# Eight modulation chunks of the second layer move into its mixing, and the dots between the gathers' begin and the gates get a larger share of each tile

## The chip, the cores and the metric

The kernel runs on one core of one Trainium2 chip. The metric is the device time of one execution in microseconds. The kernel before takes 1582.73 us, the median of three runs (1582.06 to 1584.29).

Five engines work side by side, each on a list of its own in a fixed order: PE (matrix products), DVE (vectors), ACT (functions of one argument, copies), POOL and SP (here both mostly send transfers). An instruction that waits holds everything behind it on its engine. Transfers sent by SP, ACT and POOL run in three queues, which the profile calls q1, q10 and q0.

## The reference, cut to what matters

Two layers work on 256 tokens of 1024 numbers. A layer mixes tokens, then sends each token to a few single-neuron experts:

```python
c_act = jax.nn.silu(c)
for l in range(DEPTH):                      # 2 layers
    mod = c_act @ w_ada[l] + b_ada[l]       # w_ada[l]: 1024 x 6144
    sh1, sc1, g1, sh2, sc2, g2 = split(mod, 6)
    h  = rms_norm(x, norm1_g) * (1 + sc1) + sh1
    x  = x + g1 * (mixers(h @ w_in) @ w_out)
    h2 = rms_norm(x, norm2_g) * (1 + sc2) + sh2
    # 8 heads choose 16 of 16384 experts for every token
    u   = expert_down[experts];  act = gelu(einsum('td,thkd->thk', h2, u))
    x   = x + g2 * einsum('thk,thkd->td', gate * act, expert_up[experts])
```

The modulation vector `mod` depends on `c` alone. In the kernel, `w_ada[l]` is 48 chunks ("columns") of 128x1024 numbers, 512 KB each; a chunk is multiplied by `c_act` and summed along its rows, which gives 128 entries of `mod`. Columns 24 to 31 are `sh2`.

## The kernel before, in words

A layer goes through four stages. **Mixing**: 16 chunks of `w_in` and 8 of `w_out` run through PE in split precision (a chunk becomes a high part on ACT and a low part on DVE, L270), and the small work of the mixers is placed between the chunks by a table. **Retrieval**: 16 chunks of `w_pq` give the scores, and DVE picks the best experts in many small steps, which reach into the next stage. **Down**: for the dense tokens (the first 168 in layer 0, the first 160 in layer 1) the kernel goes through all 128 tiles of `expert_down`, 8 matmuls a tile (L357). **Up**: 128 tiles of `expert_up` in the same way (L1173). Each tile is 512 KB.

The other 88 (layer 0) or 96 tokens (layer 1) don't take part in that. For them POOL gathers rows: one indirect transfer (`fetch`, L1074) brings 128 rows of `expert_down`, 512 KB, into a free place; DVE multiplies it with the tokens and sums ("dot", `dot`, L1084), which frees the place for the next gather. There is one dot for each of the 88 or 96. In the up stage the same happens with rows of `expert_up`, which DVE adds to sums ("add", `add_row`, L1097 and L1099). At the end of the up stage PE folds these sums into the result (`folds`, L1179), and DVE writes the new x (L392).

**The gates.** The dense tokens need a gate for each expert. Once the picks of a layer are known and normalised (DVE, L922 to L924), PE transposes them (L934), ACT and DVE turn them into `parts` and `picks` (L939 to L943), and then 42 groups in layer 0, 40 in layer 1, each of 4 tokens, follow: DVE compares (`compare`, L1107), ACT scales (`factors`, L1117 to L1123), PE multiplies (`gate_mm`, L1133), and DVE and ACT use the result (`gate_use`, L1143 and L1141). Two groups can be in work at a time: the compare of group g+2 stands on DVE behind the `gate_use` of group g. A group is started every second tile.

**The order of the work** in the down stage is written out by the loop over its 128 tiles, in the second half of `experts`. Before the picks are known, each tile gets a budget of small steps ("fills", `run_fill`). "Begin" is the tile at which the first picks are known and the gathers begin; "start" is the tile at which the first compares are issued (the gates follow FLUSH tiles later). From D_FIRST tiles behind begin each tile gets a share of dots, `due`: DOT_SLOW between begin and the end of the fills, DOT_FAST from there to start, DOT_RATE behind it. While the gathers run, the budget of fills is cut by 1.2 * DOT_SLOW. DVE's list is thus a mix of fills, dots and gate steps in the order in which this loop issues them, and it doesn't depend on when a gather lands.

**Transfers.** `Src.seq` lists all streamed chunks. SP sends half the tiles of the down and up stages and ACT the other half (kind "second"), into a ring of seven places (`RAW`, tile "raw"). Some tiles of the down stage are loaded early into places of their own (kind "early", `AHEAD_AT`). All 48 modulation chunks of layer 1 are "asides": SP loads them into six other buffers, and DVE dots them (`ada_chunk`, L227) when it comes to them. 40 of these, columns 0 to 39, come in the down and up stages of layer 0: six at tile 20 of the down stage, then one every five tiles of it (`ASIDES_AT`), and the last 18 spread over the up stage. The other eight come in the down stage of layer 1. SP also sends some tables for the mixing of layer 1 and reads x back (`x_dram`), both in the up stage of layer 0. POOL's queue holds the gathers.

**Places.** The dots and gathers use places of the arena that are free then. Places of "early" tiles join them when the tile is used (from `AHEAD_AT` 28 on); some of them must be given back when few fills are left (RETIRE).

Of the kernel before, what the change touches and what calls it, by code (L numbers as in the profile page):

```python
# [14 lines left out]
OP = mybir.AluOpType  # L15
# [4 lines left out]
S = 256  # L20
DC = 8
D = 1024
# [26 lines left out]
SETS_KNOWN = 22  # L49
D_FIRST = 8  # L50
DOT_SLOW = 0.3
DOT_RATE = (0.85, 0.92)
DOT_FAST = 1.6
RETIRE = 9
AHEAD_AT = (8, 12, 16, 36, 40, 44, 48, 52, 56, 60, 64, 68, 100, 28, 32)
# [3 lines left out]
AHEAD_FIRST = 4  # L59
ASIDES_AT = ((20,) * 6 + tuple(range(46, 125, 5)), (20,) * 6 + (60, 72))  # L60
ASIDES_UP = (4, 100)
F_FIRST = 4
F_LAST = 124
# [19 lines left out]
def hybrid_trunk(ctx: ExitStack, tc: tile.TileContext, x_in, c_in, vec_in, w_ada, w_in, w_out, w_pq,  # L83
# [118 lines left out]
    def dma_ahead(upto):  # L202
        while Src.loaded < min(upto, len(Src.seq)):
            kind, src, raw = Src.seq[Src.loaded]
            if kind == "aside":
                raw = stream.tile([P, D], F32, name="aside", tag=("hi", "lo")[Src.aside % 2], bufs=3)
                Src.aside += 1
            elif kind != "early":
                raw = stream.tile([P, D], F32, name="raw", tag="raw", bufs=RAW)
            if kind == "second":  # L210
                Src.later.append((Src.loaded, raw, src))
            else:
                nc.sync.dma_start(raw, src)
            raws[Src.loaded] = raw
            Src.loaded += 1
# [32 lines left out]
    def cast_step(late=None):  # L248
# [8 lines left out]
        Src.cast += 1  # L257
        if kind == "aside":
            Src.asides.append((k, lambda: ada_chunk(arg[0], arg[1], raw)))
# [46 lines left out]
    def mix(a, b, first=0, last=None):  # L306
        last = len(a) if last is None else last
        o, used = list(a[:first]), 0
        for n, t in enumerate(a[first:]):
            o.append(t)  # L310
            want = min(len(b), len(b) * (n + 1) // max(1, last - first))
            o += b[used:want]
            used = want
        return o + b[used:]

    def mats(src, layer, n, kind="mat"):
        return [(kind, src[layer, p], None) for p in range(n)]

    seq = []
    for layer in range(DEPTH):  # L320
# [3 lines left out]
        if layer == 0:  # L324
# [7 lines left out]
            body = first[:2] + body[:n] + first[2:] + mix(body[n:], ada(0, [2, 3, 4]))  # L332
        body += mix(tail[:6], ada(0, [5])) + tail[6:] if layer == 0 else tail
        seq += body + [("whole" if n in WHOLE_PQ else "mat", w_pq[layer, n], None) for n in range(16)]
        dn, un = ([t if n % 2 else ("second", *t[1:]) for n, t in enumerate(mats(w, layer, 128, "whole"))]
                  for w in (down, up))
        for n, at in enumerate(AHEAD_AT):
            dn[AHEAD_FIRST + n] = ("early", dn[AHEAD_FIRST + n][1], region(at * S, D))
        aside = ada(1, [0, 1, 2, 3, 4] if layer + 1 < DEPTH else [5], "aside")
        for n, at in reversed(tuple(enumerate(ASIDES_AT[layer]))):  # L340
            dn.insert(at, aside[n])
# [5 lines left out]
    for t in seq:  # L347
        Src.ring.append(Src.ring[-1] + was if Src.ring else 0)
        was = t[0] not in ("early", "aside")
    Src.ring.append(Src.ring[-1] + was)  # L350
# [657 lines left out]
    def experts(layer, rest):  # L1008
# [225 lines left out]
        for i in range(128):  # L1234
# [34 lines left out]
            if start is None:  # L1269
                run_fill(FILL_DOWN[layer] if begin is None else FILL_DOWN[layer] - 1.2 * DOT_SLOW)  # L1270
            if known:
# [29 lines left out]
            n = i - AHEAD_FIRST  # L1301
            if 0 <= n < len(AHEAD_AT) and AHEAD_AT[n] >= 28:
                assert not retired
                free.append(region(AHEAD_AT[n] * S, D))
                if AHEAD_AT[n] != KEPT:
                    passing.append(free[-1])
                fetch()
# [130 lines left out]
```

## Time and profile before

| what | value |
|---|---|
| median of three runs | 1582.73 us |
| the profiled execution's own time | 1584.51 us |
| its span in the trace | 1582.6 us |
| mean granted PE clock | 0.991 |
| busy share of PE, DVE, ACT, POOL | 97%, 63%, 30%, 31% |
| mean transfer rate over the span | 361 GB/s |

The stages of the profiled execution: the tiles of layer 0's down stage begin near 195 us, while DVE is still picking, and end at 509 us; its up stage runs to 824 us; in layer 1 the down stage begins near 985 us, and the up stage runs from 1286 to 1578 us.

In the profile's rows, times are in us from the span's start. A group of instructions is shown by line, engine, operation and tiles (out<-in), then busy time and mean ns of one, then the idle time of its engine just ahead of it and what ended that. A row of a timeline has start, duration, engine, line and operation, the number of instructions that it joins, and in brackets the idle time ahead of it with its releaser. In a table of windows the number in brackets behind a busy time is a count of instructions, PEclk is the granted clock of PE (1.00 is full speed), and the last two columns are the busy share of the transfer engines and the rate.

### The profile page before, as it was taken

To read this page: it belongs to the slowest core of one execution; us is meant where nothing else is said; L and a number is where in the kernel's file an instruction comes from. 1 tells how busy PE (TensorE), PEld (TensorE's weight loads), DVE (VectorE), ACT (ScalarE), POOL (GpSimd) and SP (SyncE) were. 2 spreads that over 40 slices of the span, in tenths; PEclk is the share of its full clock that TensorE was granted. 3 is DMA by queue.
4 is the path that set the end of the run, shared out by engine and by line. 5 is a ranking of instruction groups with operands and counts; after the bars stand their busy time and mean duration, and the time that the engine had idled before them with its cause. 6 is when DMAs were issued, how large, how long until landed. Compare 5 with 4: busy or idle time off the path is not lost.

```text
span 1582.6 us, 28957 instructions
## 1 busy us (share of the span) xinstructions
PE 1542.3 (97%) x11240; PEld 1505.1 (95%) x11240; DVE 1000.0 (63%) x2255; ACT 472.5 (30%) x1356; POOL 496.8 (31%) x424
## 2 busy tenths in 40 slices
PE   6999999999999999998999999999999999999997
PEld 5879999999999999998999899999999999999997
DVE  6778898677787444444337578877667754444434
ACT  2346313465553000000026663134656610000000
POOL 1000124334344434444200001245443334444441
PEclk9999999999999999999999999999999999999998
DMA  9998489999999999999955574899999999999995
GB/s 385 339 375 319 138 289 348 418 418 419 417 418 416 415 419 419 418 419 419 412 189 171 186 258 139 292 351 419 417 418 419 418 419 419 418 419 419 419 418 211
DMA packets 156681, 571.21 MB, mean 361 GB/s; under 512 B 18131, under 2 KB 18659, under 8 KB 155392
## 3 DMA queue, kind: packets, MB, share of 16 engines
q1 hardware_dynamic: 66096, 241.07, 39.7%
q0 software_dynamic: 55744, 202.36, 32.0%
q10 hardware_dynamic: 34704, 125.93, 19.9%
q8 instruction: 88, 1.44, 0.3%
q14 instruction: 49, 0.40, 0.1%
HBM read 564.02 MB, written 4.09 MB: 359 GB/s over the span
## 4 chain that ended last, share of the span: by engine, by line
PE 40%; DMA 38%; issue 8%; DVE 7%; POOL 4%; ACT 2%; ACTq 0%; POOLq 0%; SPq 0%; DVEq 0%
DMA arena<-in_up,arena 17%; PE acc L1173 17%; DMA arena<-in_down_rows,arena 12%; PE ch L357 9%; DMA spots<-in_down_rows,arena 3%; DMA raw<-in_up 3%; POOL arena L1074 3%; PE ch L359 2%; PE ch L360 2%; PE ch L361 2%; DVE raw L227 1%; DMA raw<-in_w_ada 1%; PE ch L446 1%; DVE arena L1084 1%; PE g L952 1%
## 5 line engine op out<-in xcount | busy, mean ns | idle before, releaser
L1173 PE MATMUL acc<-arena,raw 128*128 128x168 f32 (+1 forms) x4096 | 580.5, 305 | 9.0 <-DMA raw<-in_up 9.0
L1173 PEld LDWEIGHTS acc<-arena,raw 128*128 128x128 f32 x4096 | 577.6, 192 | 11.3 <-DMA raw<-in_up 11.2
L357 PE MATMUL ch<-arena,raw 128*128 128x168 f32 (+2 forms) x3776 | 560.7, 307 | 0.1
L357 PEld LDWEIGHTS ch<-arena,raw 128*128 128x128 f32 x3776 | 536.2, 190 | 5.6 <-issue 1.8
L1099 DVE SCALAR_TENSOR_TENSOR spots<-arena,spots 128x1024 f32<-128x1024 f32 x156 | 200.4, 1284 | 222.1 <-DMA arena<-in_up,arena 220.8
L1074 POOL DMA_INDIRECT arena<-in_up,arena x159 | 215.1, 1353 | 280.5 <-DMA arena<-in_up,arena 203.9
L1074 POOL DMA_INDIRECT arena<-in_down_rows,arena x151 | 178.3, 1181 | 242.9 <-DVE arena L1084 180.7
L1084 DVE SCALAR_TENSOR_TENSOR arena<-arena,spots 128x1024 f32<-128x1024 f32 x151 | 183.1, 1222 | 86.1 <-DMA arena<-in_down_rows,arena 79.6
L1117 ACT ACTIVATE arena<-arena,parts 128x128 f16<-128x128 f16 x164 | 64.6, 394 | 142.1 <-DVE arena L1107 102.5
L388 ACT ACT_TABLE_LOAD x6 | 7.7, 1283 | 284.9 <-PE acc L1173 284.8
L357 PE MATMUL ch<-arena 128*128 128x160 f32 (+2 forms) x544 | 86.0, 317 | 6.1 <-issue 3.6
L357 PEld LDWEIGHTS ch<-arena 128*128 128x128 f32 x544 | 79.8, 192 | 11.2 <-ACT arena L410 5.2
L1150 ACT ACTIVATE arena<-ch 128x336 f32<-128x336 f32 (+32 forms) x122 | 41.9, 343 | 149.4 <-PE ch L357 128.9
L227 DVE SCALAR_TENSOR_TENSOR aside<-aside,arena 128x1024 f32<-128x1024 f32 x48 | 58.6, 1220 | 43.9 <-DMA aside<-in_w_ada 43.8
L359 PE MATMUL ch<-hh,hi 128*128 128x256 f32 x288 | 82.6, 289 | 2.0 <-DVE arena L477 1.9
L360 PE MATMUL ch<-hh,lo 128*128 128x256 f32 x288 | 81.8, 284 | 0.0
L361 PE MATMUL ch<-hh,hi 128*128 128x256 f32 x288 | 81.7, 284 | 0.0
L270 DVE TENSOR_TENSOR lo<-raw,hi 128x1024 fp32r<-128x1024 f32 x42 | 51.2, 1225 | 37.3 <-ACT hi L277 36.3
L227 DVE SCALAR_TENSOR_TENSOR raw<-raw,arena 128x1024 f32<-128x1024 f32 x48 | 57.9, 1217 | 8.9 <-DMA raw<-in_w_ada 5.4
L1119 ACT ACTIVATE arena<-arena,parts 128x128 f16<-128x128 f16 x164 | 63.4, 387 | 0.0
L1123 ACT ACTIVATE arena<-arena,parts 128x128 f16<-128x128 f16 x164 | 63.4, 386 | 0.0
L1121 ACT ACTIVATE arena<-arena,parts 128x128 f16<-128x128 f16 x164 | 63.4, 386 | 0.0
(231 smaller groups left out, 1661.9 us busy)
## 6 DMA issues: line engine op xcount, KB each, us to landing
raw<-in_up SPq DMA_DIRECT2D x128, 512.0 KB
raw<-in_up ACTq DMA_DIRECT2D x128, 512.0 KB
raw<-in_down SPq DMA_DIRECT2D x114, 512.0 KB
raw<-in_down ACTq DMA_DIRECT2D x112, 512.0 KB
raw<-in_w_ada SPq DMA_DIRECT2D x48, 512.0 KB
aside<-in_w_ada SPq DMA_DIRECT2D x48, 512.0 KB
raw<-in_w_pq SPq DMA_DIRECT2D x32, 512.0 KB
arena<-in_down SPq DMA_DIRECT2D x30, 512.0 KB
```

The source lines that it names most:

```text
L227: nc.vector.scalar_tensor_tensor(raw, raw, 1.0, cact, op0=OP.mult, op1=OP.mult, accum_out=mods[layer][:, col:col + 1])
L357: nc.tensor.matmul(dst, hi[:, cols], k[0], start=start, stop=stop, **kw)
L359: nc.tensor.matmul(dst, hi[:, cols], k[0], start=start, stop=False, **kw)
L360: nc.tensor.matmul(dst, lo[:, cols], k[0], start=False, stop=False, **kw)
L361: nc.tensor.matmul(dst, hi[:, cols], k[1], start=False, stop=stop, **kw)
L1074: nc.gpsimd.indirect_dma_start(out=held[n], out_offset=None, in_=rows if n >= TS else down_rows[:, :], in_offset=bass.IndirectOffsetOnAxis ...
L1084: nc.vector.scalar_tensor_tensor(row, row, 1.0, R_DX[which(k)[0]], op0=OP.mult, op1=OP.mult, accum_out=R_DOTS[:, k:k + 1])
L1099: nc.vector.scalar_tensor_tensor(R_SUM[s], row, w, R_SUM[s], op0=OP.mult, op1=OP.add)
L1117: nc.scalar.activation(og[0][:, 0, i, :], oh[:, 0, i, :], AF.Copy, scale=parts[:, 0, t + i:t + i + 1])
L1119: nc.scalar.activation(og[1][:, 0, i, :], oh[:, 0, i, :], AF.Copy, scale=parts[:, 1, t + i:t + i + 1])
L1121: nc.scalar.activation(og[0][:, 1, i, :], oh[:, 1, i, :], AF.Copy, scale=parts[:, 0, t + 2 + i:t + 3 + i])
L1173: nc.tensor.matmul(acc[d // 2][:, (d % 2) * S:(d % 2) * S + T], u[:, d * P:(d + 1) * P], acts[:, i, :], start=i == 0 and d % 2 == 0, stop= ...
```

## The change: what it does

Columns 24 to 31 of layer 1 are no asides any more. They get the kind "inline" and stand in the list of layer 1's mixing, behind its chunks 10, 11 and 14. POOL sends them (L208 in the numbering of the change) into places of the arena, and DVE dots them there (L264) when the mixing comes to them. Two of them, columns 27 and 28, land in places that are free early, and their transfers come into POOL's list in the up stage of layer 0, behind 50 and 56 of its gathers; their dots stand on DVE among the adds, behind 46 and 47 of them. The other six come on POOL behind the last gather. On DVE column 24's dot stands ahead of the updates of x, 25's ahead of the reciprocal of the following norm and 26's behind it, and 29, 30 and 31 in the mixing.

The asides of layer 0 fall from 40 to 32: one every seven tiles of the down stage (18 there instead of 22) and 14 instead of 18 in the up stage.

The other numbers change the loop of the down stage, in both layers: DOT_SLOW from 0.3 to 0.9 dots a tile, D_FIRST from 8 to 7, RETIRE from 9 to 4, and two places fewer join the gathers (threshold 36 instead of 28). The fills keep their full budget until the first dots, and then it is 2.2 - 1.2 * 0.9 = 1.12 a tile in layer 0 instead of 2.2 - 0.36 = 1.84.

```diff
-D_FIRST = 8
-DOT_SLOW = 0.3
+D_FIRST = 7
+DOT_SLOW = 0.9
...
-RETIRE = 9
+RETIRE = 4
...
-ASIDES_AT = ((20,) * 6 + tuple(range(46, 125, 5)), (20,) * 6 + (60, 72))
+ASIDES_AT = ((20,) * 6 + tuple(range(46, 125, 7)), (20,) * 6 + (60, 72))
...
+MIXED = ((24, 10, 76), (25, 10, 80), (26, 10, 84), (27, 11, 29), (28, 11, 33), (29, 11, 37), (30, 11, 41), (31, 14, 17))
...
-            if kind == "aside":
+            if kind == "inline":
+                raw = raw[0]
+                nc.gpsimd.dma_start(raw, src)
+            elif kind == "aside":
...
-            else:
+            elif kind != "inline":
                 nc.sync.dma_start(raw, src)
...
-        if kind == "aside":
+        if kind == "inline":
+            view = (lambda v: v.rearrange("p (a b) -> p a b", a=2)) if len(raw.shape) == 3 else (lambda v: v)
+            nc.vector.scalar_tensor_tensor(raw, raw, 1.0, view(cact), op0=OP.mult, op1=OP.mult,
+                                           accum_out=mods[arg[1]][:, arg[2]:arg[2] + 1])
+            ada_end(arg[1], arg[2], 8)
+        elif kind == "aside":
...
+        body = [t for n, b in enumerate(body) for t in [b] + beside(layer, n)]
...
+        aside = [t for t in aside if t[2][1] not in apart]
...
-                run_fill(FILL_DOWN[layer] if begin is None else FILL_DOWN[layer] - 1.2 * DOT_SLOW)
+                if begin is None or i < begin + D_FIRST:
+                    run_fill(FILL_DOWN[layer])
+                elif fills[0]:
+                    run_fill(FILL_DOWN[layer] - 1.2 * DOT_SLOW)
+                else:
+                    run_aside()
...
-            if 0 <= n < len(AHEAD_AT) and AHEAD_AT[n] >= 28:
+            if 0 <= n < len(AHEAD_AT) and AHEAD_AT[n] >= 36:
```

What this does to the engines' lists is seen best in layer 1. Here is DVE's list of the kernel before around the normalisation of the picks (L922 to L924); L1084 is a dot, L902 to L912 are the last steps of the picking:

```order
L912 TENSOR_TENSOR arena<-arena 128x128
L902 TENSOR_TENSOR arena<-arena,iota_87 128x2048
L907 TENSOR_TENSOR arena<-arena 128x2048
L911 TENSOR_TENSOR arena<-arena 128x8x128
L911 TENSOR_TENSOR arena<-arena 128x8x64
L911 TENSOR_TENSOR arena<-arena 128x8x32
L912 TENSOR_TENSOR arena<-arena 128x128
L1084 SCALAR_TENSOR_TENSOR arena<-arena,spots 128x1024
L922 TENSOR_REDUCE arena<-arena 128x8
L923 RECIPROCAL arena<-arena 128x8
L924 TENSOR_TENSOR arena<-arena 128x128
```

And here is the same place after the change, where these lines have numbers higher by 22 (a dot is L1106):

```order
L924 TENSOR_TENSOR arena<-arena,iota_87 128x2048
L1085 TENSOR_SCALAR arena<-pairs 128x32
L1106 SCALAR_TENSOR_TENSOR arena<-arena,spots 128x1024
L929 TENSOR_TENSOR arena<-arena 128x2048
L1106 SCALAR_TENSOR_TENSOR spots,arena<-spots 128x1024
L1106 SCALAR_TENSOR_TENSOR arena<-arena,spots 128x1024
L933 TENSOR_TENSOR arena<-arena 128x8x128
L933 TENSOR_TENSOR arena<-arena 128x8x64
L933 TENSOR_TENSOR arena<-arena 128x8x32
L934 TENSOR_TENSOR arena<-arena 128x128
L1106 SCALAR_TENSOR_TENSOR arena<-arena,spots 128x1024 x2
L944 TENSOR_REDUCE arena<-arena 128x8
```

Dots now stand between the steps: in the whole list 18 dots come ahead of the normalisation of layer 1 instead of 3, and 16 instead of 3 in layer 0.

The second place is DVE's list up to the first `gate_use` (L1143) of layer 1, first before, from the compares (L1107) of the first two groups on:

```order
L1107 TENSOR_TENSOR arena<-iota_85,picks 128x1024 x2
L1084 SCALAR_TENSOR_TENSOR arena<-arena,spots 128x1024 x2
L227 SCALAR_TENSOR_TENSOR aside,mod_112<-aside,arena 128x1024
L1084 SCALAR_TENSOR_TENSOR arena<-arena,spots 128x1024 x6
L227 SCALAR_TENSOR_TENSOR aside,mod_112<-aside,arena 128x1024
L1084 SCALAR_TENSOR_TENSOR spots,arena<-spots 128x1024
L1084 SCALAR_TENSOR_TENSOR arena<-arena,spots 128x1024 x2
L1143 SCALAR_TENSOR_TENSOR arena<-arena,g 128x42x4
L1107 TENSOR_TENSOR arena<-iota_85,picks 128x1024
```

and after the change, where L1129 is a compare, L231 an aside's dot and L1165 a `gate_use`:

```order
L1129 TENSOR_TENSOR arena<-iota_85,picks 128x1024 x2
L1106 SCALAR_TENSOR_TENSOR arena<-arena,spots 128x1024 x4
L231 SCALAR_TENSOR_TENSOR aside,mod_112<-aside,arena 128x1024
L1106 SCALAR_TENSOR_TENSOR arena<-arena,spots 128x1024
L1106 SCALAR_TENSOR_TENSOR spots,arena<-spots 128x1024
L1106 SCALAR_TENSOR_TENSOR arena<-arena,spots 128x1024
L231 SCALAR_TENSOR_TENSOR aside,mod_112<-aside,arena 128x1024
L1106 SCALAR_TENSOR_TENSOR spots,arena<-spots 128x1024
L1106 SCALAR_TENSOR_TENSOR arena<-arena,spots 128x1024 x2
L1165 SCALAR_TENSOR_TENSOR arena<-arena,g 128x50x4
L1129 TENSOR_TENSOR arena<-iota_85,picks 128x1024
```

Counted from the layer's first dot, 32 dots stand ahead of the first `gate_use` of layer 1 instead of 19, and 28 instead of 18 in layer 0; the compare of the third group comes right behind it in both.

The third place is PE's list around the two transposes of the picks (L934) in layer 1, where a tile is 8 matmuls of L357, before:

```order
L934 MATMUL g<-ident,arena 128x128 x3
L357 MATMUL ch<-arena 128x160 x32
L357 MATMUL ch<-arena,raw 128x160 x128
L934 MATMUL g<-ident,arena 128x128 x3
L357 MATMUL ch<-arena,raw 128x160 x64
L1133 LDWEIGHTS arena
```

and after the change:

```order
L956 MATMUL g<-ident,arena 128x128 x3
L379 MATMUL ch<-arena 128x160 x32
L379 MATMUL ch<-arena,raw 128x160 x184
L956 MATMUL g<-ident,arena 128x128 x3
L379 MATMUL ch<-arena,raw 128x160 x72
L1155 LDWEIGHTS arena
```

The second transposes move back by 56 matmuls, 7 tiles, and the first gate by one tile more. In layer 0 they move from 112 to 160 matmuls behind the tiles of the same row, 6 tiles, with 8 tiles from there to the first gate as before.

More of the change, by code (lines that the diff above doesn't have):

```diff
@@ L317, in mats, with mixed, beside @@
         return [(kind, src[layer, p], None) for p in range(n)]
+    def mixed(col, at):
+        if at == 90:
+            raw = region(at * S, 2 * D).rearrange("p (a b) -> p a b", a=2)[:, :, :D // 2]
+        else:
+            raw = region(at * S, D)
+        return ("inline", w_ada[1, col], (raw, 1, col))
+    def beside(layer, n):
+        return [mixed(col, at) for col, m, at in MIXED if layer == 1 and m == n]
+    apart = [col for col, _, _ in MIXED]
     seq = []
@@ L348, in hybrid_trunk @@
         Src.ring.append(Src.ring[-1] + was if Src.ring else 0)
-        was = t[0] not in ("early", "aside")
+        was = t[0] not in ("early", "aside", "inline")
     Src.ring.append(Src.ring[-1] + was)
@@ L1269, in experts @@
             if start is None:
-                run_fill(FILL_DOWN[layer] if begin is None else FILL_DOWN[layer] - 1.2 * DOT_SLOW)
+                if begin is None or i < begin + D_FIRST:
+                    run_fill(FILL_DOWN[layer])
+                elif fills[0]:
+                    run_fill(FILL_DOWN[layer] - 1.2 * DOT_SLOW)
+                else:
+                    run_aside()
             if known:
```

## The prediction

> **What bounds the kernel now.** I begin with the busy shares and the costliest groups of the page.
>
> ```profile
> PE 1542.3 (97%) x11240; PEld 1505.1 (95%) x11240; DVE 1000.0 (63%) x2255; ACT 472.5 (30%) x1356; POOL 496.8 (31%) x424
> ...
> L1173 PE MATMUL acc<-arena,raw 128*128 128x168 f32 (+1 forms) x4096 | 580.5, 305 | 9.0 <-DMA raw<-in_up 9.0
> L357 PE MATMUL ch<-arena,raw 128*128 128x168 f32 (+2 forms) x3776 | 560.7, 307 | 0.1
> L1099 DVE SCALAR_TENSOR_TENSOR spots<-arena,spots 128x1024 f32<-128x1024 f32 x156 | 200.4, 1284 | 222.1 <-DMA arena<-in_up,arena 220.8
> ```
>
> PE is busy for 1542.3 of 1582.6 us, so its 40 us of idle time are all that a new order could win at full clock. DVE's adds wait 220.8 us for gathers, so DVE has time and transfers don't. Next the two long stretches as windows, with the short one between the layers:
>
> ```profile
> 255.00:780.00 525.00, 516.20 (x3758) 510.67 (x3757) 310.84 (x478) 134.27 (x475) 206.90 (x164) 0.99 1.03 418
> 1050.00:1555.00 505.00, 502.14 (x3841) 498.62 (x3840) 283.18 (x411) 127.27 (x454) 222.03 (x177) 1.00 1.03 418
> 820.00:830.00 10.00, 10.00 (x58) 9.35 (x58) 6.86 (x17) 5.46 (x15) 0.00 (x0) 0.94 0.39 114
> ```
>
> In the long stretches the transfer engines are full (share 1.03, 418 GB/s) and PE is nearly full too. A piece of 512 KB (a tile, an aside, a gather) costs 524288 B / 418 GB/s = 1.254 us of transfer there; between the layers (114 GB/s) there is room. Then what PE waits for:
>
> ```profile
> PE acc L1173 <- DMA raw<-in_up: 9.0, 7, 3.5
> ...
> PE acc L1179 <- DVE spots L1099: 4.5, 1, 4.5
> ...
> PE g L1133 <- ACT arena L1117: 1.9, 2, 1.3
> ```
>
> So up tiles that come late cost 9.0 us, the last add ahead of the folds 4.5, and the gates 1.9. The change touches all three.
>
> **The up stage of layer 0.** Windows of 10 us show where its waits lie, the queues from 560 to 680 us why, and the transfers sent by SP from 680 to 760 us what joins them:
>
> ```profile
> 680.00:690.00 10.00, 8.97 (x63) 8.71 (x63) 5.00 (x5) 0.00 (x0) 4.28 (x3) 1.00 1.03 420
> 690.00:700.00 10.00, 9.44 (x66) 9.19 (x66) 5.00 (x5) 0.00 (x0) 4.28 (x3) 1.00 1.03 417
> ...
> 730.00:740.00 10.00, 6.46 (x34) 6.20 (x33) 4.82 (x6) 0.00 (x0) 4.16 (x3) 0.83 1.03 415
> 740.00:750.00 10.00, 8.36 (x57) 7.84 (x55) 4.50 (x7) 0.00 (x0) 3.92 (x4) 1.00 1.02 419
> 750.00:760.00 10.00, 8.46 (x47) 8.46 (x48) 5.20 (x5) 0.00 (x0) 3.95 (x4) 0.83 1.03 420
> ```
> ```profile
> q0 software_dynamic: 5007, 18.24, 37.2%
> q1 hardware_dynamic: 5009, 18.24, 37.2%
> q10 hardware_dynamic: 3750, 13.63, 27.9%
> ```
> ```profile
> arena<-in_rel_bias SPq DMA_DIRECT2D x1, 1024.0 KB
> arena<-x_dram SPq DMA_DIRECT2D x1, 1024.0 KB
> ...
> arena<-in_sgu_w SPq DMA_DIRECT2D x1, 256.0 KB
> arena<-in_sgu_b SPq DMA_DIRECT2D x1, 128.0 KB
> ```
>
> The idle time is 1.03 + 0.56 + 3.54 + 1.64 + 1.54 = 8.3 us, and the clock of 0.83 in two windows costs 2 x 0.17 x 10 = 3.4 more: 11.7 us. SP's q1 and POOL's q0 get the same 18.24 MB, while ACT's q10 takes only its tiles. So q1 is held at 18.24 MB / 120 us = 2.90 pieces per 10 us. SP wants 13.63 MB / 120 us = 2.17 of tiles, and asides: 18 over 96 tiles of 2.34 us (L1173 runs for 300 us a layer, 128 tiles) are 0.80, together 2.97. It falls behind, and the tables (2432 KB, 4.75 pieces, 16 us of q1 at its share) come on top. Afterwards 14 asides want 0.62, together 2.79, below the share: the waits ahead of the tables go (1.6 us), and the tables meet a full ring of seven places. I estimate that this covers half of their 16 us, so of the other 10.1 us a little over half goes as well: -1.6 - 5.7 = **-7.3**; bounds -11.7 (all goes) and -1.6 (the tables cost as before). Columns 27 and 28 come back here on POOL: 2 x 1.254 = 2.5 us more in q0, and DVE stands at their dots with adds behind them. The adds have slack in layer 0 (PE waits for none at its folds), so this is 0.
>
> The Trainium skill, DMA: Bandwidth & Descriptors (rules for kernel authors), says that spreading transfers over SP, ACT and GpSimd doesn't help bandwidth, since all end on the same 16 engines. The equal 18.24 MB show that here the queue still decides who waits; by that rule alone only bytes count, six pieces fewer at 1.254 us, and the sum would have -7.5 in place of -7.3.
>
> **The gates of layer 0.** PE's rows around the second transposes and the first gates, and DVE's of dots number 16 and 17, counted from the layer's first:
>
> ```profile
> 268.70 0.49 PE L934 MATMUL g<-ident,arena 128*128 128x128 f32 x3
> ...
> 287.27 0.63 PE L1133 MATMUL g<-arena 128*128 128x128 f16 x8
> ...
> 292.35 0.62 PE L1133 MATMUL g<-arena 128*128 128x128 f16 x8
> ```
> ```profile
> 283.09 1.22 DVE L1084 SCALAR_TENSOR_TENSOR arena<-arena,spots 128x1024 f32<-128x1024 f32 x1 [1.78 <-DMA arena<-in_down_rows,arena]
> ...
> 285.91 1.23 DVE L1084 SCALAR_TENSOR_TENSOR arena<-arena,spots 128x1024 f32<-128x1024 f32 x1 [1.59 <-issue]
> ```
>
> A tile takes (287.27 - 268.70 - 0.33) / 8 = 2.28 us, two tiles with a gate 5.08. The dots wait for their gathers, and the queue is full, so DVE can't make them sooner. The change puts the third gate at 287.27 + 6 x 2.28 + 2 x 5.08 = 311.1. Its compare stands behind the first use, which stands behind 28 dots. By 287.3 about 17.4 gathers have landed; the third gate needs 10.6 more. In the meantime PE uses 10 more tiles and one aside is loaded: 21.6 pieces x 1.254 = 27.1 us, so the last gather lands near 314.4. Behind it come its dot (1.15), the use (0.25) and 2.4 for the compare and the factors (from the layer 1 rows below, compare at 1085.09, last gate part at 1087.48): 318.2, that is 7.1 late. Three groups later the same count gives 8.1, and from there the asides that are saved keep up with it. Nothing hides this: the gates stand in PE's own list. **+8**; bounds 0 (gathers come sooner than I count) and +11.
>
> **The gates of layer 1.** The same rows:
>
> ```profile
> 1057.41 0.49 PE L934 MATMUL g<-ident,arena 128*128 128x128 f32 x3
> ...
> 1075.13 0.62 PE L1133 MATMUL g<-arena 128*128 128x128 f16 x8
> ...
> 1079.99 0.62 PE L1133 MATMUL g<-arena 128*128 128x128 f16 x8
> ...
> 1086.32 0.52 PE L1133 MATMUL g<-arena 128*128 128x128 f16 x2 [1.30 <-ACT arena L1117]
> 1087.48 1.16 PE L1133 MATMUL g<-arena 128*128 128x128 f16 x6 [0.65 <-ACT arena L1117]
> ```
> ```profile
> 1075.28 1.23 DVE L1084 SCALAR_TENSOR_TENSOR arena<-arena,spots 128x1024 f32<-128x1024 f32 x1 [1.58 <-DMA arena<-in_down_rows,arena]
> ...
> 1081.18 1.22 DVE L1084 SCALAR_TENSOR_TENSOR arena<-arena,spots 128x1024 f32<-128x1024 f32 x1 [1.74 <-DMA arena<-in_down_rows,arena]
> ...
> 1085.09 0.68 DVE L1107 TENSOR_TENSOR arena<-iota,picks 128x1024 f16<-128x1024 f16 x1
> ```
> ```profile
> 1080.00:1090.00 10.00, 7.99 (x56) 7.06 (x54) 7.54 (x15) 3.15 (x11) 5.17 (x5) 0.87 1.03 421
> 1560.00:1570.00 10.00, 5.49 (x31) 5.35 (x29) 5.47 (x5) 0.00 (x0) 0.00 (x0) 0.76 0.14 59
> ```
>
> Here before already has the stall: the third gate waits 1.30 + 0.65 us for a compare that stands behind 19 dots, and the clock of 0.87 adds 1.3 and a little behind it: 3.6 in all. With the change the transposes stand at 1057.41 + 0.33 + 15 x 2.18 = 1090 less the 8 tiles before = 1072.7, but the normalisation waits for dot 18, which before began at 1081.18: a first stall of about 8 us. Then the third gate needs 32 dots. By 1075.2 16 have landed; 16 gathers, 12 tiles and one aside are 29 pieces, 36.4 us, so 1111.5, and with 3.8 behind it 1115.3, where without waits the gate would stand at 1075.13 + 8 x 2.18 + 2 x 4.86 = 1102.3: 13.0 late, of which I take 12.3 (the aside may fall outside). Less the 3.6 of before that is +8.7. At the end part comes back: the transfers run on while PE stands, the last add keeps its time, and so the 4.5 us of waiting at the folds go, with about 1.2 of the 2.4 that the clock of 0.76 behind it costs. 8.7 - 5.7 = **+3.0**; bounds -4 (the gathers come in time, the wait at the folds goes) and +9 (nothing comes back).
>
> On the clock the row of 0.87 shows that two waits of 1.30 and 0.65 us were enough for a slow phase. The Trainium skill, TensorE: Matmul & The Clock Gate (Part 1), asks for an idle window of about 3.4 us; by it such short waits would cost no clock and the 3.6 of before would be near 2, the sum 1.6 higher.
>
> **Between the layers.** Six transfers go where there is room; DVE's rows there:
>
> ```profile
> 829.18 0.17 DVE L376 RECIPROCAL rn<-rn 128x2 f32<-128x2 f32 x1 [0.73 <-ACT rn L375]
> ...
> 830.30 1.28 DVE L481 TENSOR_TENSOR arena<-arena,g 128x512 f32<-128x512 f32 x2 [0.96 <-PE g L382]
> ```
>
> One dot ahead of the reciprocal fills its 0.73 us of waiting and delays it by about 0.4; one behind it fills the 0.96. A dot is 1.22, so +0.4 to +0.7 on the path to the first products; the other three stand beside mixing work of which I can't see the slack: **+1.0**, bounds 0.4 and 4 (3 x 1.22 on the path).
>
> **The sum.** 8 - 7.3 + 3.0 + 1.0 = +4.7 against the profiled execution's 1584.51 (span 1582.6, 1.9 outside), that is 1589.2. That execution lies 1.8 above the median, so against 1582.73 it is 1587.4.
>
> **The rivals.** *The gathers come in time.* Earlier dots free places earlier, and fewer asides leave q0 more; if it then brings more than I count, the gates are met and only the gain is left: -7.3 + 1.0, and -4 in layer 1 from the folds: 1572 to 1578, say 1575. It decides if the dots of layer 0 reach number 28 by 307.3. Against it: q0 is full from 255 us on and its dots wait now. For it: my count carries one rate over 27 and 36 us. *The up stage keeps its waits.* If the tables and x alone make them, -1.6 stands in place of -7.3: 1593. For it: 10.1 of the 11.7 us lie behind the tables. *It cancels.* Stalls in the down stage let the transfers run ahead, so the up stage gets more than I gave it: -11.7 in place of -7.3, and 0 for layer 1: 1580.0 to 1583, no change.
>
> **How the numbers follow.** A measurement of this kernel tells 0.2% (3.2 us) from no change. The forecast has 0.48, with a range of its own from 1580 to 1594: 0.04 of it faster, 0.14 the same, 0.30 slower. Gathers in time 0.25, faster. The up stage keeps its waits 0.15, slower. Cancelled 0.12: 0.10 the same, 0.02 faster. Together faster 0.31, the same 0.24, slower 0.45. The range for 8 in 10 runs from 1574 (most of the first rival) to 1596 (the second with the upper bound between the layers).
>
> **What would show it.** Right: PE waits for ACT's factors (L1117, now L1139) at the third gates, together some 8 and 4 us, and for the transposes' picks in layer 1, near 8 us; waits for up tiles fall from 9.0 to about 4; no wait at the last folds. Wrong: gate waits near the 1.9 of now, or up waits still near 9.

## The result, and the profile after

The change is slower: 1602.78 us (median of 4 runs, 1600.28 to 1606.51) against 1583.09 us before in the same session, a ratio of 1.0126 with a 95% interval of 1.0103 to 1.0149. The forecast was 1587.4 us with a range from 1574 to 1596, so the change lies outside it. The direction was right, the size was not: +19.7 us where +4.7 was forecast. The profiled execution of the change took 1606.51 us, with a span of 1604.8 us and a clock of 0.986.

The first view to set beside before is what PE waits for:

```profile
PE g L956 <- DVE arena L934: 7.8, 1, 7.8
PE ch L379 <- ACT arena L1172: 6.5, 1, 6.5
PE g L1155 <- ACT arena L1139: 4.3, 6, 0.9
PE acc L1195 <- DMA raw<-in_up: 3.4, 2, 2.5
...
PE g L956 <- DVE arena L946: 2.6, 1, 2.6
PE g L676 <- ACT arena L671: 2.4, 2, 1.3
PE g L404 <- DVE rn L398: 2.4, 2, 1.7
```

The waits for up tiles fell from 9.0 to 3.4 us, and the wait ahead of the last folds (4.5 us before) is gone, both as forecast. Against that stand waits that before didn't have: 7.8 and 2.6 us of the transposes (L956) for DVE's picks, 6.5 us of a down tile (L379) for ACT, 2.4 us of the mixing (L676), and more waits of gates (L1155). These gate waits all lie at the ends of the two down stages (1.5 and 2.8 us); at the third gates, where the prediction put some 8 and 4 us, PE waits for nothing. The same two windows as before:

```profile
255.00:780.00 525.00, 513.46 (x3737) 509.92 (x3738) 296.16 (x453) 135.35 (x477) 198.15 (x158) 0.99 1.00 402
1050.00:1555.00 505.00, 489.13 (x3704) 482.63 (x3703) 288.39 (x426) 130.27 (x458) 225.75 (x179) 0.99 1.01 404
```

The transfers carry 402 and 404 GB/s where they carried 418: PE stood so long that the transfers ran dry in places (143 GB/s from 510 to 520 us, 266 from 1305 to 1315). Where the time went is read from the first and last start of the up products of each layer, here before (L1173) and after (L1195):

```profile
L1173 PE MATMUL acc<-arena,raw x2048: 306/306/627, 509.5 to 823.4; 128*128 128x168 f32 x187
L1173 PE MATMUL acc<-arena,raw x2048: 299/299/614, 1285.8 to 1578.1; 128*128 128x160 f32 x187
```
```profile
L1195 PE MATMUL acc<-arena,raw x2048: 306/306/627, 522.7 to 828.8; 128*128 128x168 f32 x187
L1195 PE MATMUL acc<-arena,raw x2048: 296/299/401, 1317.6 to 1600.3; 128*128 128x160 f32 x187
```

Layer 0's up stage begins 13.2 us late and ends 5.4 late, layer 1's begins 31.8 late and ends 22.2 late. With the first down tile of layer 1 (976.9 before, 990.2 after), the change breaks into five steps, and every experiment below can be set beside them. All numbers are us against the profiled execution of before, each from one profiled execution; that of the change lies 3.7 above its median, so its steps add up to 22.3 and not to 19.7. How far a step repeats is seen from e5 and e12, which are one and the same kernel: their rows differ by up to 1.8 us. In e9, which comes out at the time of before, the steps differ from before's by 2 to 4.5 us, so smaller numbers in those columns are not read. The step of the mixing repeats far better (0.0 in ten rows), and there 2.6 us are read. Inside a step I follow from tile to tile how late PE is against before: between two events that number stays the same over dozens of tiles, so jumps of 1 us can be seen there.

| profiled execution | layer 0 up to the end of down | layer 0 up | mixing, retrieval of layer 1 | layer 1 down | layer 1 up and folds |
|---|---|---|---|---|---|
| the change | +13.3 | -7.9 | +7.9 | +18.6 | -9.6 |
| e1, chunks moved, old loop | -3.9 | -8.7 | +7.2 | +3.8 | +1.0 |
| e2, new loop alone | +15.1 | -1.1 | 0.0 | +18.8 | -10.7 |
| e3, chunks left out, old loop | -0.2 | -7.0 | 0.0 | -1.0 | -0.1 |
| e5, six chunks in early places, old loop | -2.5 | -6.5 | 0.0 | +1.1 | -0.7 |
| e6, seven chunks, place 17 given up, old loop | -3.1 | -8.0 | +2.6 | -0.6 | +0.3 |
| e4, gates six tiles later | +10.8 | +0.3 | 0.0 | +2.9 | -4.5 |
| e7, dots ahead, budget as before | +6.5 | +0.6 | 0.0 | +9.1 | -10.6 |
| e8, budget cut, dots as before | +2.2 | +1.7 | 0.0 | 0.0 | +4.3 |
| e9, places only | -2.5 | -3.2 | 0.0 | -2.1 | +4.5 |
| e10, e5 with `DOT_FAST` 0.8 | -4.8 | -4.6 | 0.0 | -1.5 | +3.8 |
| e11, the change, six chunks in early places | +8.4 | -4.5 | 0.0 | +16.2 | -10.9 |
| e12, e5 once more | -3.7 | -6.2 | 0.0 | +1.7 | +1.1 |

**The first gates of layer 0.** DVE and then PE after the change; L965 makes `parts`, L1129 the compares, L1106 is a dot, L231 an aside's dot:

```profile
294.53 1.23 DVE L1106 SCALAR_TENSOR_TENSOR arena<-arena,spots 128x1024 f32<-128x1024 f32 x1 [1.72 <-DMA arena<-in_down_rows,arena]
...
295.68 1.22 DVE L231 SCALAR_TENSOR_TENSOR aside<-aside,arena 128x1024 f32<-128x1024 f32 x1
...
296.83 0.28 DVE L965 SCALAR_TENSOR_TENSOR parts<-g,arena 128x128 f32<-128x128 f32 x1
297.03 1.28 DVE L1129 TENSOR_TENSOR arena<-iota,picks 128x1024 f16<-128x1024 f16 x2
```
```profile
297.80 0.40 ACT L1139 ACTIVATE arena<-arena,parts 128x128 f16<-128x128 f16 x1 [9.94 <-DVE arena L1129]
...
302.49 0.76 ACT L1172 ACTIVATE arena<-ch 128x336 f32<-128x336 f32 x2
```
```profile
302.97 9.49 PE L379 MATMUL ch<-arena,raw 128*128 128x168 f32 x48 [6.48 <-ACT arena L1172]
```

The compares come behind 21 dots, the last of which waits for its gather until 294.5. ACT stands at the factors (L1139) for 9.94 us, and the activation of the next down tiles (L1172) stands behind them, so PE has no free bank and stops for 6.48 us, in plain tiles and before the first gate. The cause is the one that the prediction named, dots that wait for gathers ahead of gate steps; the place is not. The first gate then comes at 312.30 and the third at 322.5, without a wait: the 28th dot began at 310.07, while PE was late already.

**The first gates of layer 1.** PE's three transposes (L956) before the gates, and the last dot that they wait for:

```profile
1095.96 0.48 PE L956 MATMUL g<-ident,arena 128*128 128x128 f32 x1 [7.83 <-DVE arena L934]
1099.01 0.47 PE L956 MATMUL g<-ident,arena 128*128 128x128 f32 x1 [2.57 <-DVE arena L946]
```
```profile
1092.96 1.23 DVE L1106 SCALAR_TENSOR_TENSOR arena<-arena,spots 128x1024 f32<-128x1024 f32 x1 [1.45 <-DMA arena<-in_down_rows,arena]
```

PE stands for 10.4 us, first for the last picking step (L934), then for the normalisation (L946); the prediction expected about 8 there and 4 more at the third gate, which waits for nothing.

**The end of the down stages.** The last groups of layer 1 on PE, with two tiles at full clock ahead of them, and the window around them:

```profile
1293.13 4.56 PE L379 MATMUL ch<-arena,raw 128*128 128x160 f32 x32
...
1300.22 0.28 PE L1155 MATMUL g<-arena 128*128 128x128 f16 x2
1301.13 1.10 PE L1155 MATMUL g<-arena 128*128 128x128 f16 x6 [0.63 <-ACT arena L1139]
...
1304.35 0.41 PE L1155 MATMUL g<-arena 128*128 128x128 f16 x2
1305.40 1.11 PE L1155 MATMUL g<-arena 128*128 128x128 f16 x6 [0.64 <-ACT arena L1139]
...
1309.62 0.52 PE L1155 MATMUL g<-arena 128*128 128x128 f16 x2 [0.88 <-ACT arena L1139]
1310.77 1.16 PE L1155 MATMUL g<-arena 128*128 128x128 f16 x6 [0.64 <-ACT arena L1139]
1311.74 6.07 PE L379 MATMUL ch<-arena,raw 128*128 128x160 f32 x32
```
```profile
1305.00:1315.00 10.00, 7.83 (x43) 6.50 (x44) 2.12 (x4) 4.40 (x17) 0.00 (x0) 0.83 0.69 266
```

The last four groups of each layer stand one tile apart, not two. G_LAST is still 124, but the gates begin six to eight tiles later, and 42 groups two tiles apart need 84 tiles. A tile and a gate take 2.7 us (2.18 and 0.46), but the next group needs use, compare and factors first, and the groups come 4.1 and 5.3 us apart here (1300.22, 1304.35, 1309.62). PE waits little at a time (0.6 to 0.9 us), but the clock falls to 0.83 in this window, and 32 products take 6.07 us (4.56 at 1293.13). From the start of tile 118 to the first up product, layer 1's down stage is 8.4 us longer than before and layer 0's 5.2. In both, 1.4 us of it are three groups more (0.46 us each), which before stood at the front. The rest in layer 1: waits of 2.8 us, the clock of 0.83 over 10 us, which is 1.7, and 2.5 that I can't place. In layer 0: waits of 1.5, the same clock from 510 to 520 us, 1.7, and 0.6. The prediction has no term for this.

**The mixing of layer 1.** POOL's sends of the moved chunks, DVE's dots of columns 25 and 31 (L264) with what stands behind them, and PE:

```profile
829.43 1.07 POOL L208 DMA_DIRECT2D arena<-in_w_ada  x2 [21.60 <-PE acc L1195]
...
858.82 0.53 POOL L208 DMA_DIRECT2D arena<-in_w_ada  x1 [14.06 <-ACT rq L397]
```
```profile
835.60 1.23 DVE L264 SCALAR_TENSOR_TENSOR arena<-arena 128x1024 f32<-128x1024 f32 x1 [1.52 <-DMA arena<-in_w_ada]
...
836.75 0.16 DVE L398 RECIPROCAL rn<-rn 128x2 f32<-128x2 f32 x1
...
864.26 1.23 DVE L264 SCALAR_TENSOR_TENSOR arena<-arena 128x1024 f32<-128x1024 f32 x1 [5.14 <-DMA arena<-in_w_ada]
...
866.55 0.47 DVE L608 SCALAR_TENSOR_TENSOR arena<-arena,vec,g 128x256 f32<-128x256 f32 x1
```
```profile
836.96 1.22 PE L404 MATMUL g<-ident,rn 128*128 128x128 f32 x4 [1.73 <-DVE rn L398]
```

Column 25's transfer can only be sent when the last up tile has been used (place 80), and it lands some 6 us later; DVE waits for it ahead of the reciprocal that PE needs. Column 31's waits for place 17, is sent at 858.82 and lands at 864.2; behind its dot stand a low part and the norm of the keys (L608). PE waits 1.7 us at L404, 2.4 at L676 and 0.8 at L381 there, of which before has none. The granted clock has a share as well:

```profile
836.00:841.00 5.00, 4.04 (x14) 3.50 (x14) 4.87 (x11) 1.71 (x4) 0.00 (x0) 0.66 0.19 76
...
914.00:920.00 6.00, 5.86 (x35) 5.66 (x36) 1.62 (x4) 1.36 (x3) 0.00 (x0) 0.72 0.41 128
```

Before has 1.00 in both windows. 0.34 x 5 and 0.28 x 6 are 1.7 us each, and 4.9 + 3.4 = 8.3 is about the step of +7.9 us.

### The profile page after: what moved, and what is told of

It is laid out like the page before. It is cut to its first block, busy times and chain, and to the rows that moved or that the text cites. A ratio compares the mean times of both kernels' runs of the same rounds, so it can differ in the third digit from the quotient of the medians.

```text
span 1604.8 us, 28956 instructions
## 1 busy us (share of the span) xinstructions
PE 1548.6 (96%) x11240; PEld 1510.1 (94%) x11240; DVE 996.7 (62%) x2248; ACT 470.1 (29%) x1353; POOL 501.7 (31%) x432
## 4 chain that ended last, share of the span: by engine, by line
PE 64%; DMA 20%; DVE 8%; issue 4%; ACT 3%; POOL 1%; ACTq 0%; SPq 0%; DVEq 0%; POOLq 0%
PE acc L1195 33%; PE ch L379 17%; DMA arena<-in_down_rows,arena 11%; DMA spots<-in_down_rows,arena 2%; DMA raw<-in_up 2%; PE ch L381 2%; PE ch L382 2%; DMA spots<-dot_in 2%; PE ch L383 2%; PE g L1155 1%; DVE arena L1106 1%; DMA raw<-in_w_ada 1%; POOL arena L1096 1%; DVE raw L231 1%; PE acc L383 1%
## 5 line engine op out<-in xcount | busy, mean ns | idle before, releaser
L1195 PE MATMUL acc<-arena,raw 128*128 128x168 f32 (+1 forms) x4096 | 575.9, 304 | 3.9 <-DMA raw<-in_up 3.4
L1195 PEld LDWEIGHTS acc<-arena,raw 128*128 128x128 f32 x4096 | 574.2, 191 | 4.9 <-DMA raw<-in_up 3.9
L379 PE MATMUL ch<-arena,raw 128*128 128x168 f32 (+2 forms) x3776 | 567.4, 310 | 9.3 <-ACT arena L1172 6.5
L379 PEld LDWEIGHTS ch<-arena,raw 128*128 128x128 f32 x3776 | 542.4, 192 | 15.5 <-ACT arena L1172 10.2
L1096 POOL DMA_INDIRECT arena<-in_up,arena x159 | 208.2, 1309 | 328.6 <-DMA arena<-in_up,arena 151.5
L1096 POOL DMA_INDIRECT arena<-in_down_rows,arena x153 | 184.8, 1208 | 222.4 <-DVE arena L1106 148.8
L1106 DVE SCALAR_TENSOR_TENSOR arena<-arena,spots 128x1024 f32<-128x1024 f32 x153 | 184.8, 1221 | 67.8 <-DMA arena<-in_down_rows,arena 63.3
L1172 ACT ACTIVATE arena<-ch 128x320 f32<-128x320 f32 (+39 forms) x126 | 44.8, 356 | 247.5 <-PE ch L379 222.7
L1165 DVE SCALAR_TENSOR_TENSOR arena<-arena,g 128x200 f32<-128x200 f32 (+20 forms) x82 | 42.6, 519 | 87.5 <-ACT arena L1163 78.6
L379 PE MATMUL ch<-arena 128*128 128x160 f32 (+2 forms) x544 | 88.2, 322 | 4.9 <-issue 3.0
L379 PEld LDWEIGHTS ch<-arena 128*128 128x128 f32 x544 | 81.9, 196 | 10.1 <-issue 4.1
L1139 ACT ACTIVATE arena<-arena,parts 128x128 f16<-128x128 f16 x164 | 64.8, 395 | 78.7 <-DVE arena L1129 59.7
L381 PE MATMUL ch<-hh,hi 128*128 128x256 f32 x288 | 82.4, 288 | 1.9 <-DVE arena L499 1.9
L231 DVE SCALAR_TENSOR_TENSOR aside<-aside,arena 128x1024 f32<-128x1024 f32 x40 | 48.8, 1220 | 45.3 <-DMA aside<-in_w_ada 38.2
L1143 ACT ACTIVATE arena<-arena,parts 128x128 f16<-128x128 f16 x164 | 64.0, 390 | 0.0
L231 DVE SCALAR_TENSOR_TENSOR raw<-raw,arena 128x1024 f32<-128x1024 f32 x48 | 57.9, 1217 | 8.9 <-DMA raw<-in_w_ada 5.3
```

What stands on the lines that cost most here:

```text
L231: nc.vector.scalar_tensor_tensor(raw, raw, 1.0, cact, op0=OP.mult, op1=OP.mult, accum_out=mods[layer][:, col:col + 1])
L379: nc.tensor.matmul(dst, hi[:, cols], k[0], start=start, stop=stop, **kw)
L381: nc.tensor.matmul(dst, hi[:, cols], k[0], start=start, stop=False, **kw)
L1096: nc.gpsimd.indirect_dma_start(out=held[n], out_offset=None, in_=rows if n >= TS else down_rows[:, :], in_offset=bass.IndirectOffsetOnAxis ...
L1106: nc.vector.scalar_tensor_tensor(row, row, 1.0, R_DX[which(k)[0]], op0=OP.mult, op1=OP.mult, accum_out=R_DOTS[:, k:k + 1])
L1139: nc.scalar.activation(og[0][:, 0, i, :], oh[:, 0, i, :], AF.Copy, scale=parts[:, 0, t + i:t + i + 1])
```

## Experiments

**Which half makes the loss?** e1 keeps the moved chunks and takes the loop back, e2 is the other half, e3 leaves the eight chunks out altogether.

```diff
# e1_moved_only, against the change
-D_FIRST = 7
-DOT_SLOW = 0.9
-RETIRE = 4
+D_FIRST = 8
+DOT_SLOW = 0.3
+RETIRE = 9
...
+                run_fill(FILL_DOWN[layer] if begin is None else FILL_DOWN[layer] - 1.2 * DOT_SLOW)
...
+            if 0 <= n < len(AHEAD_AT) and AHEAD_AT[n] >= 28:
```

> The change with the loop of the down stage as before (0.3 dots a tile, D_FIRST 8, RETIRE 9, the old budget, threshold 28): only the eight chunks are moved and the asides thinned. Theory (the loop makes the loss): the up stage of layer 0 gains 8 us, and the mixing of layer 1 loses 8 us, because DVE waits there for columns 25 and 31; together 1580 to 1586, and no gate waits beyond the 1.9 us of before. Rival (the moved chunks make the loss, through POOL's queue and the places): 1595 to 1605, with the gates late as in the change.

Measured: 1583.86 us, ratio 1.0004 (0.9988 to 1.0020). As the theory had it: -8.7 in the up stage, +7.2 in the mixing, gate waits of 1.5 us. The theory has nothing for the +3.8 in layer 1's down stage, where PE waits once for 3.4 us for ACT (L1175); e5 and e6 don't repeat it.

e2_loop_only is the kernel before with the other side of the same lines: the four numbers and the budget of the change.

> The kernel before with the loop of the change alone (0.9 dots a tile, D_FIRST 7, RETIRE 4, the new budget, threshold 36); all 40 asides stay. Theory (the loop makes the loss): layer 0's down stage is 13 us or more longer, layer 1's 19, some 10 come back at the last folds: 1602 to 1610. Rival (the moved chunks): 1583 to 1590.

Measured: 1602.66 us, ratio 1.0128 (1.0104 to 1.0153), the whole loss of the change. Its waits, with before's line numbers:

```profile
PE g L934 <- DVE arena L912: 11.5, 2, 10.7
PE acc L1173 <- DMA raw<-in_up: 8.9, 7, 3.0
...
PE g L934 <- DVE arena L924: 6.8, 2, 4.2
PE g L1133 <- ACT arena L1117: 5.3, 8, 0.9
```

The up tiles wait 8.9 us as before (9.0), so stalls in the down stage don't let the transfers of the up stage run ahead. That speaks against the rival "it cancels".

```diff
# e3_left_out, against e1
-MIXED = ((24, 10, 76), (25, 10, 80), (26, 10, 84), (27, 11, 29), (28, 11, 33), (29, 11, 37), (30, 11, 41), (31, 14, 17))
+MIXED = ()
...
-    apart = [col for col, _, _ in MIXED]
+    apart = list(range(24, 32))
+    nc.vector.memset(mods[1][:, 24:32], 0.0)
```

> The same as e1_moved_only, but the eight chunks are neither loaded nor dotted (the second shift of layer 1 is set to zero). Theory: what is left of the move is its gain, the 8 us in layer 0's up stage, and nothing is lost in the mixing of layer 1: 1573 to 1577. Rival (the gain comes from the down stage's stalls, which let transfers run ahead, not from the asides): 1581 to 1583.

Measured: 1573.69 us, ratio 0.9936 (0.9916 to 0.9957). Without this shift the kernel isn't whole, but it shows the gain alone: eight asides fewer are worth 7.0 us in the up stage and about 8 in all, and nothing else moves clearly. The two halves add up: steps of e1 plus e2 give 11.2, -9.8, 7.2, 22.6, -9.7, together 21.5 where the change has 22.3.

**What in the loop?** e4 moves only the gates (FLUSH 6 to 12 in the kernel before). e7 and e8 split the change's loop: e7 cuts the budget by 0.36 a tile as before, so that the dots stand ahead but the first gate stays at its tile; e8 keeps 0.3 dots a tile and cuts the budget by 1.08, so that the gates slip without the dots. e9 changes only the places.

```diff
# e4_late_gates, against before
-FLUSH = 6
+FLUSH = 12
# e7_dots_not_budget, against e2
-                    run_fill(FILL_DOWN[layer] - 1.2 * DOT_SLOW)
+                    run_fill(FILL_DOWN[layer] - 0.36)
# e8_budget_not_dots, against e2
-DOT_SLOW = 0.9
+DOT_SLOW = 0.3
-                    run_fill(FILL_DOWN[layer] - 1.2 * DOT_SLOW)
+                    run_fill(FILL_DOWN[layer] - 1.08)
# e9_places_only, against before
-RETIRE = 9
+RETIRE = 4
-            if 0 <= n < len(AHEAD_AT) and AHEAD_AT[n] >= 28:
+            if 0 <= n < len(AHEAD_AT) and AHEAD_AT[n] >= 36:
```

> The kernel before with FLUSH 12 in place of 6: the same dots ahead of the picks' normalisation, but the first gate six tiles later in each layer, so that the last groups stand one tile apart at the end, as in the change. Theory (groups one tile apart can't be followed by compare and factors): 4 us more at the end of layer 0's down stage and 8 at the end of layer 1's, of which some 6 come back at the last folds: 1586 to 1592. Rival (the bunch costs nothing, only the dots ahead of the normalisation do): 1579 to 1584.

Measured: 1593.56 us, ratio 1.0071 (1.0046 to 1.0096). Layer 0 loses 5.0 us at the third gate and 8.4 at its end. Layer 1 gains 4.8 where before's third gate waits, loses 9.0 at its own third gate, and only 1.5 at its end, where the last three groups stand one tile apart and not four. So a third gate does wait here, as the prediction had it for the change. It isn't the clean test that it was meant to be: with the gates later, 23 and 25 dots come ahead of the first use, which the expectation left out.

> As e2_loop_only, but the budget of the fills is cut by 0.36 a tile as before, not by 1.08: the dots stand ahead of the gate steps (9 ahead of each normalisation, 24 and 26 ahead of the first use) while the first gate stays at its tile of before, so nothing bunches at the end. Theory (dots ahead of gate steps make PE wait for gathers): 8 us in each layer at the first gates, of which some 6 come back at the last folds, nothing at the ends of the down stages: 1587 to 1595. Rival (only the late gates and their bunch cost): 1580 to 1584.

Measured: 1589.91 us, ratio 1.0042 (1.0025 to 1.0059). PE stands for 6.9 us behind ACT at the first compares of layer 0 (L357 for L1150, as in the change), and for 3.8 + 3.2 + 2.5 us in layer 1. Against before, layer 0 loses 9.8 us at the first gates, and nothing that can be read at the end of its down stage; layer 1's down stage loses 9.1, and 10.6 come back at the folds. Dots ahead of gate steps cost by themselves, with nothing bunched.

> As e2_loop_only, but with 0.3 dots a tile as before and only the budget cut by 1.08: the gates begin six to eight tiles later and bunch at the end, with 5 dots ahead of each normalisation and 19 ahead of the first use. Theory (bunched gates cost by themselves): 5 to 7 us at the end of each down stage, nothing at the first gates (layer 1 even saves the 3.6 us of before), some 5 back at the last folds: 1584 to 1592. Rival (the dots ahead make all of the loss): 1579 to 1583.

Measured: 1589.86 us, ratio 1.0042 (1.0028 to 1.0056). The last groups of layer 0 on PE:

```profile
498.20 0.32 PE L1133 MATMUL g<-arena 128*128 128x128 f16 x2
499.16 1.11 PE L1133 MATMUL g<-arena 128*128 128x128 f16 x6 [0.65 <-ACT arena L1117]
500.11 2.50 PE L357 MATMUL ch<-arena,raw 128*128 128x168 f32 x16
503.50 0.52 PE L1133 MATMUL g<-arena 128*128 128x128 f16 x2 [0.89 <-ACT arena L1117]
504.66 1.16 PE L1133 MATMUL g<-arena 128*128 128x128 f16 x6 [0.64 <-ACT arena L1117]
```

The bunch is there, with waits like those of the change: from tile 118 on, 8.2 us at the end of layer 0's down stage, 4.0 at the end of layer 1's (the clock stays at 1.00 there), and none at the first gates (layer 1 even gains 5 there). Layer 1's step of 0.0 hides this, since a down tile that comes late near tile 30 costs 4.7 as well. So the bunch costs by itself too. What failed is the expectation for the folds. With fewer dots early, dots and adds end later (layer 1's last dot begins at 1296.7 us instead of 1286.6, its last add at 1572.6 instead of 1564.3), and the last wait grows from 4.5 to 10.1 us:

```profile
PE acc L1179 <- DVE spots L1099: 10.1, 1, 10.1
```

> The kernel before with RETIRE 4 and the threshold 36 alone: two places fewer join the gathers and the others are given back later. Theory (the transfer queue is full, so places don't set when a gather lands): no change, 1580 to 1586. Rival (fewer places starve the gathers): dots and gates late, 1587 to 1592.

Measured: 1582.07 us, ratio 1.0000 (0.9985 to 1.0014). Fewer places don't change the time. The steps of this one execution differ from before's by 2 to 4.5 us both ways.

**What in the mixing?** e5 moves six chunks into places that are free early, e6 seven and gives up only place 17; both have the old loop.

```diff
# e5_six_early, against e1
-MIXED = ((24, 10, 76), (25, 10, 80), (26, 10, 84), (27, 11, 29), (28, 11, 33), (29, 11, 37), (30, 11, 41), (31, 14, 17))
+MIXED = ((26, 10, 76), (27, 11, 29), (28, 11, 33), (29, 11, 37), (30, 11, 41), (31, 14, 84))
# e6_not_seventeen, against e1
+MIXED = ((25, 10, 80), (26, 10, 84), (27, 11, 29), (28, 11, 33), (29, 11, 37), (30, 11, 41), (31, 14, 76))
```

> As e1_moved_only (the old loop), but only six chunks are moved, into places that are free early: columns 24 and 25 are asides again, 26 and 31 take places 76 and 84, and nothing waits for place 80 or for place 17. Theory (the 7 us in the mixing of layer 1 are DVE's waits for columns 25 and 31): they go, the gain in layer 0's up stage stays but for two asides: 1573 to 1578. Rival (any dot of a moved chunk in the mixing costs its 1.2 us there): 1580 to 1584.

> As e1_moved_only, but seven chunks are moved: column 24 is an aside again and column 31 takes place 76, so that only the late place 17 is given up; column 25 still waits for place 80. Theory: of the 7 us in the mixing the 4 that begin at column 31's dot go, the 3 ahead of the first products stay: 1577 to 1581. Rival (column 25's wait alone makes all 7): 1581 to 1585.

Measured: e5 1575.70 us, ratio 0.9950 (0.9931 to 0.9969); e6 1577.77 us, ratio 0.9965 (0.9953 to 0.9976). The step of the mixing is 0.0 in e5 and +2.6 in e6, where e1 has +7.2: place 17 costs 4.6 us, place 80 2.6. In e5 dots still stand in the mixing and the step is 0.0:

```profile
820.23 0.17 DVE L398 RECIPROCAL rn<-rn 128x2 f32<-128x2 f32 x1 [0.73 <-ACT rn L397]
...
829.43 1.23 DVE L264 SCALAR_TENSOR_TENSOR arena<-arena 128x1024 f32<-128x1024 f32 x1
...
832.85 1.22 DVE L264 SCALAR_TENSOR_TENSOR arena<-arena 128x1024 f32<-128x1024 f32 x1
```

So it isn't a dot's 1.22 us that costs but a dot that waits for a transfer into a late place.

> The change with its own loop, but six moved chunks in early places, as in e5_six_early. Theory (the two costs add up: the mixing's waits go, the gates' stay): 7 or 8 us less than the change, 1593 to 1598. Rival (the waits in the mixing are hidden behind the late gates, or the other way round): 1600 to 1605.

Measured (the change with e5's MIXED): 1593.93 us, ratio 1.0063 (1.0038 to 1.0088), some 9 us less than the change, which has 7.9 in the mixing. The two costs add up.

**Versions that beat both.** e5 and e6 do; e12 is e5 again, and e10 is e5 with `DOT_FAST = 0.8` in place of 1.6.

> e5_six_early once more, word for word, in five rounds, for its interval and beside e10_fewer_dots on one chip: 1573 to 1578, ratio 0.994 to 0.997.

> As e5_six_early with DOT_FAST 0.8 in place of 1.6: in layer 1 17 dots stand ahead of the first use instead of 19, 16 instead of 18 in layer 0, and all later dots come later as well. Theory (even the kernel before has too many dots ahead of layer 1's first use): 3 us less than e5_six_early, 1570 to 1575. Rival (dots that are put off come back as late adds ahead of the last folds): as e5_six_early or slower, 1575 to 1580, with a longer wait at the last folds than its 4.4 us.

Measured: e12 1575.92 us, ratio 0.9950 (0.9930 to 0.9969); e10 1574.64 us, ratio 0.9937 (0.9915 to 0.9959). The intervals overlap, so e10's dots aren't shown to gain anything. Its waits suggest why:

```profile
PE acc L1195 <- DMA raw<-in_up: 8.7, 4, 2.6
PE acc L1201 <- DVE spots L1121: 6.0, 1, 6.0
...
PE g L1155 <- ACT arena L1139: 1.1, 2, 0.6
```

The gates wait 1.1 us (3.7 in e12), but the folds 6.0 and the up tiles 8.7 (5.5 and 5.2): what is saved at the gates seems to be paid later.

## Why the prediction was wrong, point by point

| term of the sum | forecast | measured in the change | what the runs say |
|---|---|---|---|
| up stage of layer 0 | -7.3 | -7.9 | right: e3 -7.0; e2, e4, e7 and e8, with all asides, -1.1 to +1.7 |
| first gates of layer 0 | +8 | +8.1 | size near (1.9 ahead of them, 7.9 at them, 1.7 back later), in part by luck: the wait is at the first compares, not at the third gate |
| gates of layer 1 | +8.7 | +10.2 | size near: 1.6 + 12.3 - 5.3 + 1.6 along the stage; all of it at the transposes, none at the third gate |
| last folds | -5.7 | -9.6 | too small: e2 -10.7, e7 -10.6 |
| between the layers | +1.0 | +7.9 | too small: places 17 (4.6) and 80 (2.6 in e6) |
| ends of the down stages | no term | +5.2 and +8.4 | missing: the gates bunch (1.4 of each is gate work that before stood at the front) |

The measured column adds up to 22.3 where 4.7 was forecast. The error of 17.6 is made of 13.6 from the missing term, 6.9 from the mixing, 1.6 from the gates, less 0.6 and 3.9 from the up stage and the folds.

**The step that failed** is the part on the gates of the two layers: it took the first gate as late and let the last ones follow as before. The first gate of layer 0 comes behind tile 46 instead of 40, that of layer 1 behind 50 instead of 42, and G_LAST stays at 124. A two-line count would have given the bunch: 42 groups two tiles apart need 84 tiles and 78 are left, 40 need 80 and 74 are left. The 2.4 us for compare and factors, which the prediction uses itself, would have shown that a group one tile (2.18 to 2.28 us) behind another must wait. e8 shows this term alone, with 8.2 and 4.0 us.

Inside the terms on the gates the mechanism was right only in part. Dots that wait for gathers do hold the gate steps (e7), but the prediction let PE wait at the third gates, 8 us in layer 0 and 4 in layer 1. In the change the first compares of layer 0 and the transposes of layer 1 were held instead, and the third gates weren't. (One working there is slightly off: 1057.41 + 0.33 + 15 x 2.18 less 8 x 2.18 is 1073.0, not 1072.7; nothing rests on it.)

**The second step** is "between the layers". It priced a dot by its 1.22 us and bounded the term at 4. What stands behind the dots was seen for columns 24 to 26, but a transfer's own time was taken as free because there was room. e5 and e6 show that dots without a late transfer cost nothing that can be read and that a late transfer does: column 31's was sent 14.06 us after POOL came to it and landed 5.4 us later. The slow clock behind such waits, about 3.4 of the 7.9 us, had no term either.

**The rivals.** The gathers didn't come in time (e7: 9.8 and 9.1 us with the dots ahead; in the change dot number 28 began at 310.07 us, past the 307.3 at which the rival decides). The up stage didn't keep its waits (e3). It didn't cancel: in e2 and e4 the up stage of layer 0 keeps 8.5 to 8.9 us of waits (8.3 before) although its down stage ended 11 to 15 us late. Places were named as one reason for the first rival; e9 shows that they have no effect of their own on the time.

The claim on the clock held: short waits again went with a slow phase (0.83 around waits of 0.63 to 0.88 us). The claim on the queues is open. The up stage gained 4.5 to 8.7 us in every run with fewer asides (-3.2 to +1.7 with all of them), but by counting bytes alone the prediction had -7.5 against -7.3, and no run tells the two apart.

**Still open**: of the 8.4 us at the end of layer 1's down stage 2.5 are not explained, and no run changes the clock alone. That the chunks could be moved all eight without loss, with two more early places, wasn't tried.

## What to carry to other kernels

When a change shifts the start of a series of steps that has a fixed last position, count whether the steps still fit at their old spacing, and price the ones that don't by the chain from one to the next. Work put ahead of a step on an engine with a fixed order costs what its own inputs make it wait, not its duration: dots of 1.2 us each, waiting for their gathers, held PE for 6 to 10 us. A load that is moved out of a full stretch must be sent early enough; its place, and who stands behind the instruction that uses it, decide what it costs.

## What the runs showed of the hardware that wasn't expected

A transfer of 512 KB that is sent where the transfer engines aren't full still takes 5.4 us to land (column 31: sent 858.82, its dot released at 864.26, at 221 and 159 GB/s in the two windows of 10 us), and about 6 for two sent together at 829.43, where the full engines finish 512 KB every 1.254 us. And a few waits of 0.6 to 0.9 us within 12 us came with a granted clock of 0.83 over a window of 10 us (1305 to 1315 us), so that the slow products (6.07 against 4.56 us for 32) cost more than any one of the waits. The sum of the waits doesn't settle it: 1.5 us in two waits came with 0.83 at the end of layer 0 in the change (510 to 520 us) and with 1.00 at the end of layer 1 in e8 (1280 to 1290 us).
